# Rotary embedding over 16 batches: all transfers through one DMA ring, tables in 16 packets of 4 KB, slabs 2 and 3 stored as a pair

## The chip, the cores and the metric

The kernel runs on one core of a Trainium2 chip. A core has a matrix engine (PE), a vector engine (DVE, VectorE), a scalar engine (ACT, ScalarE), GpSimd (POOL) and a sync engine (SP, SyncE), and 16 DMA engines that move data between HBM and the on-chip memory of 128 partitions. SP and ACT each have a DMA ring of their own: a queue whose transfers are worked off in the order in which the engine issued them, spread over the 16 DMA engines. The metric is the device time of one execution in microseconds; the number that stands for a kernel is the median of its runs.

## What is computed

```python
batch, seq, dim = 16, 512, 1024        # num_heads = 16, head_dim = 64, half_dim = 32
x = x.reshape(batch, seq, num_heads, head_dim)
x1, x2 = x[..., :half_dim], x[..., half_dim:]
cos = cos[None, :, None, :]            # cos and sin: 512 x 32, float32
sin = sin[None, :, None, :]
rotated = np.concatenate([x1 * cos - x2 * sin,
                          x1 * sin + x2 * cos], axis=-1)   # float32
```

The input `x` is 33.55 MB and so is the output; the two tables are 64 KB each.

## The kernel before

**Tiling.** Two batches make a slab: 1024 rows of 1024 values, 4 MB. Two slabs make a pair. In a pair, partition p holds 16 consecutive rows, 64 KB; the first 32 KB belong to the even slab, the second 32 KB to the odd one. There are eight slabs and three places on chip for pairs (L52): pair 0 (slabs 0, 1) shares its place with pair 3 (slabs 6, 7), so slab 6 can be loaded only when slab 0 has been stored, and slab 7 when slab 1 has. A transfer of one slab is 128 packets of 32 KB, one of a pair 128 packets of 64 KB; `here` and `there` (L55, L59) give the two ends.

**Order of transfers.** On SP's ring stand all loads of `x`: load 0, load 1, slabs 2 and 3 as a pair in two halves (even partitions, then odd ones, L82), slabs 4 and 5 as a pair, and later, from inside the main loop (L168), load 6 and load 7. On ACT's ring stand the two tables (L78: 64 partitions of 1 KB each), and then all stores: slabs 0, 1, 2 and 3 one by one (L166), slabs 4 and 5 as a pair in two halves (L160), slabs 6 and 7 as a pair (L164). ACT issues a store between its own computing instructions.

**Tables.** GpSimd fills `pick` with zeros (L88) and sets ones or minus ones in it with four selects (L92). When the tables have landed, GpSimd casts them to bf16 (L99), PE multiplies them by `pick` (L106), which spreads the 64 rows over 128 partitions and gives the sign of the sine, and the two results `acc0` and `acc1` are cast into `tab0` on VectorE (L113) and `tab1` on ACT (L144).

**The main loop** runs over passes: slab 0 in two halves of four rows, slabs 1 to 6 whole, slab 7 in parts of 4, 2 and 2 rows. For each, ACT casts the float32 values to bf16 in the same place (L134), VectorE multiplies twice by the tables (L152) and adds (L155), and ACT copies the result back to float32 (L158). Casts run ahead of the copies: ACT's order is the cast of slab s+1, then the copy of slab s; from slab 6 on, all casts that are left come first. `copy` (L137) keeps ACT's order as written, and cast and copy both show up under L138.

Of the kernel before, what the change touches and what calls it, by code (L numbers as in the profile page):

```python
# [2 lines left out]

# [4 lines left out]


@with_exitstack  # L10
def kernel(
    ctx: ExitStack,
    tc: tile.TileContext,
    x: bass.AP,
    cos: bass.AP,
    sin: bass.AP,
    num_heads: int,
    out: bass.AP,
):
    nc = tc.nc  # L20
    P = nc.NUM_PARTITIONS

    batch, seq, dim = x.shape
    nh = num_heads
    hd = dim // nh
    half = hd // 2
    bf16 = mybir.dt.bfloat16
    f32 = mybir.dt.float32

    nb = 2  # L30
    nslabs = batch // nb
    rpp = nb * seq // P
    W = rpp * dim
    TP = seq // rpp
    TW = rpp * half

    out_flat = out.rearrange("b s h d -> b s (h d)")

    singles = ctx.enter_context(tc.tile_pool(name="singles", bufs=1))
    pairs = ctx.enter_context(tc.tile_pool(name="pairs", bufs=3))  # L40
    psum = ctx.enter_context(tc.tile_pool(
        name="psum", bufs=1, space=bass.MemoryType.PSUM))


    def view(t, offset, *dims):
        return dataclasses.replace(t, offset=t.offset + offset,
                                   ap=[t.ap[0], *[list(d) for d in dims]])

    places = [pairs.tile([P, 2 * W], f32, tag="pair", name="pair") for _ in range(3)]  # L52


    def here(s, n=1):  # L55
        return view(places[s // 2 % 3], s % 2 * W, (1, n * W))


    def there(t, s, n=1):  # L59
        return bass.AP(tensor=t.tensor, offset=t.offset + s // 2 * 2 * P * W + s % 2 * W,  # L60
                       ap=[[2 * W, P], [1, n * W]])


    def load(s, n=1):
        nc.sync.dma_start(out=here(s, n), in_=there(x, s, n))  # L65


    def store(s, n=1):
        nc.scalar.dma_start(out=there(out_flat, s, n), in_=here(s, n))  # L69


    load(0)


    cos_sb = singles.tile([TP, TW], f32, tag="cos_sb")
    sin_sb = singles.tile([TP, TW], f32, tag="sin_sb")
    for t, src in ((cos_sb, cos), (sin_sb, sin)):
        nc.scalar.dma_start(out=t, in_=bass.AP(  # L78
            tensor=src.tensor, offset=src.offset, ap=[[TW, TP], [1, TW]]))

    load(1)
    for p in range(2):  # L82
        nc.sync.dma_start(out=here(2, 2)[p::2], in_=there(x, 2, 2)[p::2])  # L83
    load(4, 2)


    pick = singles.tile([TP, 4 * P], bf16, tag="pick")
    nc.gpsimd.memset(pick, 0.0)  # L88
    for h in range(2):
        for g in range(2):  # L90
            part = view(pick, (2 * h + g) * P, (TP // 2, 2 * P // TP), (1, TP // 2))
            nc.gpsimd.affine_select(  # L92
                out=part, in_=part, compare_op=mybir.AluOpType.not_equal,
                fill=1.0 - 2.0 * g, base=-h, pattern=[[0, 2 * P // TP], [-2, TP // 2]],
                channel_multiplier=1)

    tab1 = singles.tile([TP, 2 * TW], bf16, tag="tab1")
    for i, t in enumerate((cos_sb, sin_sb)):
        nc.gpsimd.tensor_copy(out=view(tab1, i * TW, (1, TW)), in_=t)  # L99

    accs, tabs = [], []
    for h in range(2):
        acc = psum.tile([P, 2 * rpp * hd], f32, tag=f"acc{h}", name="acc")
        for i in range(2):
            for f in range(2):
                nc.tensor.matmul(  # L106
                    view(acc, i * rpp * hd + f * half, (hd, rpp), (1, half)),
                    view(pick, (2 * h + i * f) * P, (1, P)),
                    view(tab1, i * TW, (half, rpp), (1, half)),
                    start=True, stop=True)  # L110
        accs.append(acc)
        tabs.append(singles.tile([P, 2 * rpp * hd], bf16, tag=f"tab{h}", name="tab"))
    nc.vector.tensor_copy(out=tabs[0], in_=accs[0])  # L113

    passes = []
    for s in range(nslabs):
        r = 0  # L120
        for n in {0: (4, 4), nslabs - 1: (4, 2, 2)}.get(s, (rpp,)):
            passes.append((s, r, n))
            r += n


    def halves(u):
        s, r, n = u
        t = here(s).bitcast(bf16)
        return [view(t, (2 * r + i * n) * dim, (1, n * dim)) for i in range(2)]


    def cast(u):
        s, r, n = u
        copy(halves(u)[0], view(here(s), r * dim, (1, n * dim)))  # L134


    def copy(out, in_):  # L137
        tc.keep_in_program_order(nc.scalar.copy(out=out, in_=in_))  # L138


    ahead = list(passes)
    for _ in range(2):
        cast(ahead.pop(0))
    copy(tabs[1], accs[1])  # L144
    cast(ahead.pop(0))
    for i, u in enumerate(passes):
        s, r, n = u
        while ahead and len(passes) - len(ahead) < (i + 2 if s < nslabs - 2 else len(passes)):
            cast(ahead.pop(0))
        lo, up = halves(u)  # L150
        for t, a in ((up, 0), (lo, rpp * hd)):
            nc.vector.tensor_mul(  # L152
                out=t, in0=lo,
                in1=view(tabs[s % 2], a + r * hd, (hd, n), (0, nh), (1, hd)))
        nc.vector.tensor_add(  # L155
            out=up, in0=up, in1=view(lo, half, (hd, n * nh), (-half, 2), (1, half)))

        copy(view(here(s), r * dim, (1, n * dim)), up)  # L158
        if r + n == rpp:
            if s == 5:  # L160
                for p in range(2):
                    nc.scalar.dma_start(out=there(out_flat, 4, 2)[p::2], in_=here(4, 2)[p::2])  # L162
            elif s == 7:
                store(6, 2)  # L164
            elif s < 4:
                store(s)  # L166
            if s < 2:
                load(s + 6)  # L168


# [1 line left out]
_INS = ['x', 'cos', 'sin', 'num_heads']  # L172
_OUTS = [((16, 512, 16, 64), 'float32')]

_NUMBERS = {'num_heads': 16}


# [26 lines left out]
```

## Time and profile before

| | |
|---|---|
| median of 3 runs | 161.87 us (161.72 to 161.93) |
| the profiled run | 161.8 us, span 160.0 us |
| ACT casts and copies (L138) | 22 instructions, 112.1 us, 5155 ns each on average; 7.02 us for a whole slab |
| VectorE multiplies (L152) | 22 instructions, 71.4 us; 4.43 us for a whole slab |
| VectorE adds (L155) | 11 instructions, 35.8 us |
| cosine lands, cast on GpSimd | 0.74 + 11.1 us, 391 ns |
| sine lands, cast on GpSimd | 1.34 + 15.8 us, 396 ns |
| matmuls for the tables (L106) | 8, of which the last six take 1.43 us together |
| ACT starts slab 0, 1, 2, 4 | 13.35, 23.24, 44.49, 73.41 us |
| stores issued | 37.30, 58.47, 72.82, 87.38, 115.58, 116.14, 138.21 us |
| loads of slabs 6 and 7 issued | 69.8, 90.4 us |
| an issue of a DMA | 0.33 to 0.67 us on SP, 0.34 to 0.65 us on ACT |

The span is the time from the first to the last event that the profiler recorded on the core; the time of a run lies 1.8 us above it here. Stretches of the span are given in microseconds from its start. A transfer is recorded packet by packet; "lands" means the time at which its completion message arrives.

### The profile page before, as it was taken

The page shows a single profiled execution, that of the slowest core. Times are in us where ns is not written, and L with a number is a line of the kernel's source. Part 1 is how long each engine was busy: PE and PEld are TensorE (multiplying, and loading weights), DVE is VectorE, ACT ScalarE, POOL GpSimd, SP SyncE. Part 2 cuts the span into 40 slices and gives each one's busy share as a digit, 9 for nine tenths or more (in the row PEclk, how much of TensorE's full clock was granted, in tenths as well). Part 3 has the DMA queues.
Part 4 walks back from the last instruction along what each step waited for, and adds up shares of the span by engine and source line. Part 5 has one row for each costly group of instructions (what it writes and reads, how often), then busy time and mean ns, then how long its engine had stood idle before and what let it go on. Part 6 is the DMA issues. An engine that isn't in the chain of part 4 may idle for free.

```text
span 160.0 us, 167 instructions
## 1 busy us (share of the span) xinstructions
PE 2.0 (1%) x8; PEld 1.0 (1%) x8; DVE 107.9 (67%) x34; ACT 114.3 (71%) x24; POOL 2.6 (2%) x11
## 2 busy tenths in 40 slices
PE   0001300000000000000000000000000000000000
PEld 0000100000000000000000000000000000000000
DVE  0000499999951999799889979998999998000000
ACT  3006959993089989998998999999879999500000
POOL 4000000000000000000000000000000000000000
DMA  7999999699599999999999999999997999989966
GB/s 262 401 401 410 426 491 524 262 524 524 254 401 410 606 426 393 393 393 393 467 451 393 434 483 393 401 500 410 393 590 328 524 393 393 524 360 426 524 262 262
DMA packets 1920, 67.24 MB, mean 420 GB/s; under 512 B 256, under 2 KB 384, under 8 KB 384
## 3 DMA queue, kind: packets, MB, share of 16 engines
q1 hardware_dynamic: 880, 33.55, 49.5%
q10 hardware_dynamic: 1040, 33.69, 48.7%
HBM read 33.69 MB, written 33.55 MB: 420 GB/s over the span
## 4 chain that ended last, share of the span: by engine, by line
ACT 52%; DMA 26%; issue 5%; ACTq 1%; SPq 1%; another core or an unknown queue 0%
ACT pair L138 52%; DMA pair<-in_x_dram 26%; ACTq L162 1%; ACTq L69 1%; SPq L65 0%; SPq L83 0%; ACTq L138 0%
## 5 line engine op out<-in xcount | busy, mean ns | idle before, releaser
L138 ACT CAST pair<-pair 128x8192 bf16<-128x8192 f32 (+5 forms) x22 | 112.1, 5155 | 21.9 <-DMA pair<-in_x_dram 19.8
L152 DVE TENSOR_TENSOR pair<-pair,tab 128x8192 bf16<-128x8192 bf16 (+2 forms) x22 | 71.4, 3259 | 9.3 <-ACT pair L138 8.9
L155 DVE TENSOR_TENSOR pair<-pair 128x8192 bf16<-128x8192 bf16 (+2 forms) x11 | 35.8, 3260 | 0.3
L113 DVE CAST tab<-acc 128x1024 bf16<-128x1024 f32 x1 | 1.2, 1225 | 18.3 <-PE acc L106 18.3
L138 ACT ACT_TABLE_LOAD x1 | 1.3, 1283 | 2.0 <-issue 2.0
L106 PE MATMUL acc<-tab,pick 64*128 64x256 bf16 x8 | 2.0, 403 | 17.1 <-POOL tab L99 17.1
L106 PEld LDWEIGHTS <-pick 64*128 64x128 bf16 x8 | 1.0, 127 | 17.6 <-issue 15.6
L92 POOL TENSOR_SCALAR_AFFINE_SELECT pick<-pick 64x128 bf16<-64x128 bf16 x4 | 1.1, 303 | 0.1
L138 ACT CAST tab<-acc 128x1024 bf16<-128x1024 f32 x1 | 1.0, 1004 | 0.0
L99 POOL CAST tab<-cos_sb 64x256 bf16<-64x256 f32 x1 | 0.4, 391 | 9.5 <-DMA cos_sb<-in_cos_dram 9.5
L88 POOL MEMSET pick<- 64x512 bf16 x1 | 0.5, 519 | 0.3 <-POOLq L185 0.3
L99 POOL CAST tab<-sin_sb 64x256 bf16<-64x256 f32 x1 | 0.4, 396 | 4.9 <-DMA sin_sb<-in_sin_dram 4.9
L185 POOL MEMSET const-float32-0.0<- 128x1 f32 x1 | 0.1, 104 | 0.2 <-issue 0.2
L185 POOL MEMSET const-bfloat16-1.0<- 128x1 bf16 x1 | 0.1, 107 | 0.0
L185 POOL MEMSET const-uint8-127<- 128x1 uint8 x1 | 0.1, 107 | 0.0
L185 POOL MEMSET const-float32-1.0<- 128x1 f32 x1 | 0.1, 104 | 0.0
## 6 DMA issues: line engine op xcount, KB each, us to landing
pair<-in_x_dram SPq DMA_DIRECT2D x4, 4096.0 KB, 22.5
out_dram<-pair ACTq DMA_DIRECT2D x4, 4096.0 KB, 32.8
cos_sb<-in_cos_dram ACTq DMA_DIRECT2D x1, 64.0 KB, 11.1
sin_sb<-in_sin_dram ACTq DMA_DIRECT2D x1, 64.0 KB, 15.8
pair<-in_x_dram SPq DMA_DIRECT2D x3, 42.2
out_dram<-pair ACTq DMA_DIRECT2D x3, 21.0
```

The source lines that it names most:

```text
L69: nc.scalar.dma_start(out=there(out_flat, s, n), in_=here(s, n))
L88: nc.gpsimd.memset(pick, 0.0)
L92: nc.gpsimd.affine_select(out=part, in_=part, compare_op=mybir.AluOpType.not_equal, fill=1.0 - 2.0 * g, base=-h, pattern=[[0, 2 * P // TP] ...
L99: nc.gpsimd.tensor_copy(out=view(tab1, i * TW, (1, TW)), in_=t)
L106: nc.tensor.matmul(view(acc, i * rpp * hd + f * half, (hd, rpp), (1, half)), view(pick, (2 * h + i * f) * P, (1, P)), view(tab1, i * TW, ( ...
L113: nc.vector.tensor_copy(out=tabs[0], in_=accs[0])
L138: tc.keep_in_program_order(nc.scalar.copy(out=out, in_=in_))
L152: nc.vector.tensor_mul(out=t, in0=lo, in1=view(tabs[s % 2], a + r * hd, (hd, n), (0, nh), (1, hd)))
L155: nc.vector.tensor_add(out=up, in0=up, in1=view(lo, half, (hd, n * nh), (-half, 2), (1, half)))
L162: nc.scalar.dma_start(out=there(out_flat, 4, 2)[p::2], in_=here(4, 2)[p::2])
L185: nc = _bacc.Bacc("TRN2", target_bir_lowering=False, num_devices=1)
```

## The change

All transfers are issued by SP, in the order in which they stand in the program, with ACT issuing none.

- The tables are no longer laid over 64 partitions in packets of 1 KB. Each is cut into 16 rows of 4 KB, cosine in partitions 0, 8, 16, ..., sine in partitions 4, 12, 20, ... of one tile `raw` (128 partitions of 1024 float32 values), which VectorE fills with zeros first. They stand on SP's ring behind load 0 and ahead of load 1.
- GpSimd casts all of `raw` in one instruction. `pick` has 128 rows and six blocks, set by six selects. Each quarter of `acc` is now the sum of two matmuls over 128 rows, so there are 16 matmuls instead of 8.
- The load of slabs 4 and 5 moves from the start to behind store 0.
- Behind store 1 stand load 6 and load 7.
- Slabs 2 and 3 are stored as a pair, in two halves of 64 packets of 64 KB, when slab 3 is done; slabs 4 and 5 and slabs 6 and 7 as before.

So the ring's order is: load 0, cosine, sine, load 1, load 2-3 (two halves), store 0, load 4-5, store 1, load 6, load 7, store 2-3 (two halves), store 4-5 (two halves), store 6-7. The casts, multiplies, adds and copies of the main loop stay as they are.

```diff
     def load(s, n=1):
-        nc.sync.dma_start(out=here(s, n), in_=there(x, s, n))
+        tc.keep_in_program_order(nc.sync.dma_start(out=here(s, n), in_=there(x, s, n)))
     def store(s, n=1):
-        nc.scalar.dma_start(out=there(out_flat, s, n), in_=here(s, n))
+        tc.keep_in_program_order(
+            nc.sync.dma_start(out=there(out_flat, s, n), in_=here(s, n)))
+    TR = 16
+    TC = seq * half // TR
+    raw = singles.tile([P, TC], f32, tag="raw")
+    nc.vector.memset(raw, 0.0)
     load(0)
-    cos_sb = singles.tile([TP, TW], f32, tag="cos_sb")
-    sin_sb = singles.tile([TP, TW], f32, tag="sin_sb")
-    for t, src in ((cos_sb, cos), (sin_sb, sin)):
-        nc.scalar.dma_start(out=t, in_=bass.AP(
-            tensor=src.tensor, offset=src.offset, ap=[[TW, TP], [1, TW]]))
+    for i, src in enumerate((cos, sin)):
+        to = dataclasses.replace(
+            raw, offset=raw.offset + 4 * i * raw.ap[0][0],
+            ap=[[P // TR * raw.ap[0][0], TR], [1, TC]])
+        tc.keep_in_program_order(nc.sync.dma_start(out=to, in_=bass.AP(
+            tensor=src.tensor, offset=src.offset, ap=[[TC, TR], [1, TC]])))
     load(1)
     for p in range(2):
-        nc.sync.dma_start(out=here(2, 2)[p::2], in_=there(x, 2, 2)[p::2])
-    load(4, 2)
-    pick = singles.tile([TP, 4 * P], bf16, tag="pick")
+        tc.keep_in_program_order(
+            nc.sync.dma_start(out=here(2, 2)[p::2], in_=there(x, 2, 2)[p::2]))
+    pick = singles.tile([P, 6 * P], bf16, tag="pick")
     nc.gpsimd.memset(pick, 0.0)
-    for h in range(2):
-        for g in range(2):
-            part = view(pick, (2 * h + g) * P, (TP // 2, 2 * P // TP), (1, TP // 2))
+    for g in range(3):
+        for m in range(2):
+            part = view(pick, (g * 2 + m) * P + m, (2 * TR, P // TR // 2), (2, TR))
             nc.gpsimd.affine_select(
...
-    tab1 = singles.tile([TP, 2 * TW], bf16, tag="tab1")
-    for i, t in enumerate((cos_sb, sin_sb)):
-        nc.gpsimd.tensor_copy(out=view(tab1, i * TW, (1, TW)), in_=t)
+    raw_b = singles.tile([P, TC], bf16, tag="raw_b")
+    nc.gpsimd.tensor_copy(out=raw_b, in_=raw)
...
-        for i in range(2):
-            for f in range(2):
+        for g, at in ((0, 0), (0, half), (1, rpp * hd), (2, rpp * hd + half)):
+            for m in range(2):
                 nc.tensor.matmul(
-                    view(acc, i * rpp * hd + f * half, (hd, rpp), (1, half)),
-                    view(pick, (2 * h + i * f) * P, (1, P)),
-                    view(tab1, i * TW, (half, rpp), (1, half)),
-                    start=True, stop=True)
+                    view(acc, at, (hd, rpp), (1, half)),
+                    view(pick, (g * 2 + m) * P, (1, P)),
+                    view(raw_b, (2 * m + h) * TW, (half, rpp), (1, half)),
+                    start=m == 0, stop=m == 1)
...
         if r + n == rpp:
-            if s == 5:
+            if s == 7:
+                store(6, 2)
+            elif s > 1 and s % 2:
                 for p in range(2):
-                    nc.scalar.dma_start(out=there(out_flat, 4, 2)[p::2], in_=here(4, 2)[p::2])
-            elif s == 7:
-                store(6, 2)
-            elif s < 4:
+                    tc.keep_in_program_order(nc.sync.dma_start(
+                        out=there(out_flat, s - 1, 2)[p::2], in_=here(s - 1, 2)[p::2]))
+            elif s < 2:
                 store(s)
-            if s < 2:
-                load(s + 6)
+            if s == 0:
+                load(4, 2)
+            elif s == 1:
+                load(6)
+                load(7)
```

More of the change, by code (lines that the diff above doesn't have):

```diff
@@ L33 @@
     W = rpp * dim
-    TP = seq // rpp
     TW = rpp * half
@@ L92 @@
             nc.gpsimd.affine_select(
                 out=part, in_=part, compare_op=mybir.AluOpType.not_equal,
-                fill=1.0 - 2.0 * g, base=-h, pattern=[[0, 2 * P // TP], [-2, TP // 2]],
-                channel_multiplier=1)
-    tab1 = singles.tile([TP, 2 * TW], bf16, tag="tab1")
-    for i, t in enumerate((cos_sb, sin_sb)):
-        nc.gpsimd.tensor_copy(out=view(tab1, i * TW, (1, TW)), in_=t)
+                fill=-1.0 if g == 2 else 1.0, base=-4 if g else 0,
+                pattern=[[0, P // TR // 2], [-(P // TR), TR]], channel_multiplier=1)
```

## The prediction

> **What bounds the kernel now.** I read the page first: the span, engine totals and DMA rows.
>
> ```profile
> span 160.0 us, 167 instructions
> PE 2.0 (1%) x8; PEld 1.0 (1%) x8; DVE 107.9 (67%) x34; ACT 114.3 (71%) x24; POOL 2.6 (2%) x11
> ...
> DMA  7999999699599999999999999999997999989966
> ...
> q1 hardware_dynamic: 880, 33.55, 49.5%
> q10 hardware_dynamic: 1040, 33.69, 48.7%
> ```
>
> No engine passes 71%, while the packets of the two queues fill 49.5 + 48.7 = 98.2% of the 16 DMA engines' span. q1 is SyncE's ring (the loads, 33.55 MB), q10 ScalarE's (the stores and, from the 33.69, the two tables). The chain of waits hides this: it gives ACT 52% and DMA 26%, because it sees a transfer only where an engine waits for it.
>
> Then I cut the span where one row of packets ends on the first of the 16 engines and the next begins (a row: one packet on each engine). Columns: stretch, length, five engines' busy time, granted clock, DMA share, GB/s of packets that start inside.
>
> ```profile
> 1.96:3.77 1.81, 0.00 (x0) 0.00 (x0) 0.00 (x0) 1.28 (x1) 0.45 (x2) 1.00 0.51 199
> 3.77:22.62 18.85, 2.01 (x8) 0.92 (x7) 4.23 (x3) 8.02 (x3) 0.79 (x2) 1.00 1.04 440
> 22.62:39.54 16.92, 0.00 (x0) 0.00 (x0) 16.85 (x7) 14.04 (x3) 0.00 (x0) 1.00 1.02 434
> 39.54:42.52 2.98, 0.00 (x0) 0.00 (x0) 2.94 (x2) 0.00 (x0) 0.00 (x0) 1.00 0.64 242
> 42.52:119.93 77.41, 0.00 (x0) 0.00 (x0) 68.17 (x16) 72.70 (x11) 0.00 (x0) 1.00 1.01 437
> 119.93:139.29 19.36, 0.00 (x0) 0.00 (x0) 15.67 (x10) 18.24 (x7) 0.00 (x0) 1.00 1.01 437
> 139.29:160.00 20.71, 0.00 (x0) 0.00 (x0) 0.00 (x0) 0.00 (x0) 0.00 (x0) 1.00 0.87 377
> ```
>
> Loads alone (22.62 on) run at 434 GB/s, loads and stores mixed (42.52 on) at 437, stores alone (119.93 on) at 437. That is one ceiling: rings and direction don't change it. The same view cut into single rows gives the unit: a row of 64 KB packets takes 16.92 / 7 = 2.417 us, one of 32 KB 1.21.
>
> ```profile
> 17.75:18.96 1.21, 1.21 (x6) 0.57 (x4) 0.70 (x1) 1.21 (x1) 0.00 (x0) 1.00 1.01 433
> ...
> 37.13:39.54 2.41, 0.00 (x0) 0.00 (x0) 2.38 (x2) 0.14 (x1) 0.00 (x0) 1.00 1.16 435
> 39.54:42.52 2.98, 0.00 (x0) 0.00 (x0) 2.94 (x2) 0.00 (x0) 0.00 (x0) 1.00 0.64 242
> 42.52:43.73 1.21, 0.00 (x0) 0.00 (x0) 1.21 (x1) 0.00 (x0) 0.00 (x0) 1.00 1.01 433
> ...
> 136.83:139.29 2.46, 0.00 (x0) 0.00 (x0) 0.00 (x0) 1.35 (x1) 0.00 (x0) 1.00 1.05 453
> ```
>
> The sixteen slabs moved (eight in, eight out) are 64 rows of 64 KB: 64 x 2.417 = 154.7 us. All else the transfers lose is small and can be listed. (a) The first row takes 1.81 instead of 1.21: 0.60. (b) From 3.77 to 22.62 pass 15 rows of 32 KB, 15 x 1.21 = 18.15, in 18.85: the tables cost 0.70. (c) The row of loads during which the first store arrives takes 2.98 instead of 2.41: 0.57. (d) The last row before store 6-7 takes 2.46: 0.04. Sum: 1.96 + 154.7 + 0.60 + 0.70 + 0.57 + 0.04 = 158.6. The last store lands at 138.21 + 21.0 = 159.2, the span ends at 160.0, the profiled run's time is 161.8 and the median of the runs 161.87. So the change can win only out of (a) to (d), 1.9 us, and lose whatever it opens as a gap.
>
> **Part 1, the tables.** Before, 8 packets of 1 KB on each engine cost 0.70, or 0.088 each, of which 2.417 / 64 = 0.038 is data: 0.050 overhead. After, each engine gets 2 packets of 4 KB: 2 x 2.417 / 16 = 0.30 of data, and 0 to 2 x 0.050 overhead. I take the middle, 0.35: saved 0.70 - 0.35 = **0.35** (0.30 to 0.40).
>
> The Trainium skill ("DMA: Bandwidth & Descriptors", Rules for kernel authors) speaks against this: transfers under 64 KB are mostly overhead, and its fit gives about 2.0 us fixed for each DMA (for transfers from GpSimd). If both tables paid that inside the one ring, the sum would lose some 4 us. The trace goes against it where more is queued: 64 rows at 2.417, across all boundaries between transfers, leave only the 1.9 us listed.
>
> **Part 2, work for the tables.** VectorE fills `raw` at the start, and the tables' issue waits for that. No row shows this fill; bounds are POOL's 0.5 us (memset of 512 values) doubled and the 1.2 us of VectorE's L113 cast of 1024 values. Behind the wait stand the issues of the tables, load 1 and both halves of load 2-3, five of 0.4 to 0.7 us; load 0 keeps the ring full to 12.2, so the cost is 0. The masks on POOL grow from 4 selects of 303 ns to 6, and are done long before. GpSimd's cast goes from 256 values on 64 partitions (0.39 us) to 1024 on 128: four to eight times, 1.6 to 3.1. The matmuls for `acc0` go from 2 after the last cast (0.6 us) to 8, 1.9 us at the rate of the six at 17.64 (1.43 us) and 3.3 at 0.41 each. The tables land near 12.6 + 0.6 instead of 17.2, so VectorE's first multiply (19.58 now) comes between 17.9 and 20.8 (with L113's 1.2). At worst that is 1.2 late: slab 0's last add ends at 34.3 instead of 33.13, its last copy 3.6 later at 37.9 instead of 37.3, and store 0 is issued then; its ring has work to 41.6 and needs it at 40.4. Cost 0.
>
> **Part 3, one ring.** Loads 0-3 now run undisturbed to 1.96 + 1.81 + 7 x 1.21 + 0.35 + 4 x 2.417 + 8 x 2.417 = 41.6. Then, in ring order with 9.67 for a slab and 19.33 for a pair: store 0 to 51.3, load 4-5 to 70.6, store 1 to 80.3, load 6 to 89.9, load 7 to 99.6, store 2-3 to 119, store 4-5 to 138.3, store 6-7 to 157.6, all up to 0.57 later if (c) stays. What could open a gap is an issue that comes late. From issue to first row takes 1.2 us (0.74 to 1.96; 138.21 to 139.29 is 1.1), from last row to landing 0.65 (158.6 to 159.2).
>
> ACT starts slab 2 at 41.6 + 0.65 = 42.3 instead of 44.49. Two casts and copies of 13.94 each end at 56.2 (store 1, needed at 69.4) and 70.2. Slab 4 lands at 71.5 instead of 73.41, so 1.9 is won; ACT no longer pauses 0.41 to issue store 3, and slab 6's multiply starts 2.3 earlier, 106.4. From there VectorE sets the pace. Store 2-3 is ready at 85.4, needed at 98.4; store 4-5 at 113.3, needed at 117.8; store 6-7 at 138.2 - 2.3 = 135.9, needed at 137.1: the smallest margin, 1.2. SP's queue blocks once on a transfer: load 7 waits for store 1 to land, 81.0, and is needed at 88.7; behind it stand only store 2-3 and later, so nothing is held up. So (d) goes: **0.04**. Eight 64 KB rows for sixteen of 32 KB at stores 2-3 give 8 x (2 x 1.21 - 2.417), **0.02**.
>
> **Part 4, loss (c).** It ends in a load's row, while the first store's own row takes a clean 1.21. Either it comes from a store ring joining running loads; then it goes, 0.57 saved. Or it is the price of the first store; then it stays, 0 saved. The rows speak for both: the lengthened row is the load's, but in the 77.41 us after it, load 7's ring joins running stores with no such loss. No row is nearer to one end; I take half, **0.28**.
>
> **Sum.** 0.35 + 0.04 + 0.02 + 0.28 = 0.69 off: 161.87 - 0.69 = **161.2**; 160.9 if (c) goes, 161.5 if it stays.
>
> **Rivals.** *Only the tables' part comes through*: 161.5, 0.41 less. For it: a first write can be slow wherever it is queued. Against: the store's own row is not longer.
>
> *Turning round inside one ring costs.* In the trace a ring never goes from loads to stores without idling. The new ring turns three times to stores and twice back to loads (51, 80). If the engines don't fetch across a turn, each turn to a load pays the start-up of (a), 0.60, and each to a store (c)'s 0.57: 2 x 0.60 + 3 x 0.57 = 2.91, less the old 0.57 and the 0.41: +1.9, **163.8**. With only the two turns to loads: 162.1 to 162.7. It decides from 0.2 us a turn on (0.98 / 5). Against it: in the mixed stretch every engine turns at nearly each row and still makes 437 GB/s; but there another ring supplies the next packet.
>
> On this, the Trainium skill ("DMA: Bandwidth & Descriptors", Two DMAs through the same engine are not ordered) says that a queue's descriptors start in order but are pipelined, with reads and writes on separate queues. By that no turn costs; no row here shows it for a mixed ring.
>
> *The tables stop the ring.* Each now stands alone in the stream with one packet per engine, and nothing beside it. If each pays the start-up of (a), that is 2 x 0.60 = 1.2: 162.4. Against it: load 0 to load 1 and all later boundaries cost nothing visible. This is what would be left of the skill's rule.
>
> *The last store comes late.* If slab 4 lands, or the end of ACT's work comes, more than 1.2 us behind my schedule, the ring runs dry before store 6-7, and each further us costs one. With no gain over before at 138.2, the gap is 1.1: 161.2 + 1.1 = 162.3.
>
> **Chances.** Forecast (160.8 to 161.4) 0.47; only the tables' part (161.4 to 161.7) 0.26; turns 0.17; tables stop the ring 0.03; late last store 0.07. Less than 0.2%, 0.32 us, can't be told from no change here, so faster is below 161.55. Faster: 0.47 and 0.10 of the 0.26 = 0.57. Same: the other 0.16. Slower: 0.17 + 0.03 + 0.07 = 0.27. The range goes from 160.7 to 162.8, leaving out the full price of the turns and a little below, under 0.2; the forecast's own is 160.8 to 161.5.
>
> **What would show it.** Right: one DMA queue with 98% or more of the span; slab 2's cast near 42.3, slab 4's near 71.5, last copy near 136, the last store landing near 158.5. (c) is read from the row after load 2-3. Wrong: stretches around 41.6, 51, 71, 80 and 100 below 430 GB/s (turns), or a hole before the last 8 MB (late store).

## The result, and the profile after

The changed kernel takes 162.56 us (median of 9 runs, 161.95 to 163.49) against 161.87 for the kernel before (9 runs beside it, 161.72 to 162.24): ratio 1.0044, 95% interval 1.0028 to 1.006. It is slower by 0.7 us where 0.7 less was forecast. Ratios and intervals, here and below, are worked out from the fast runs alone, so a ratio need not be the quotient of the two medians beside it. The profiled run, at 161.95 us, is the fastest of the nine; two further sets of runs of the same kernel (below, `again` and `third`) left traces of 162.48 and 162.57 us, and the readings use these as well.

The page of the changed kernel: span, engine totals, the DMA engines in 40 slices, the queue, the chain's summary.

```profile
span 160.2 us, 194 instructions
PE 3.4 (2%) x16; PEld 2.3 (1%) x16; DVE 108.7 (68%) x35; ACT 114.0 (71%) x24; POOL 3.3 (2%) x12
...
DMA  7999999799699897999999999996997997997992
...
q1 hardware_dynamic: 1696, 67.24, 98.0%
...
DMA 34%; ACT 29%; DVE 12%; issue 8%; ACTq 2%; SPq 1%
```

One queue carries all, 98.0% of the span, and no slice inside is empty: nothing here looks wrong. The chain again names the DMA engines only where somebody waits for them.

The timeline, at the points that the schedule had named (start, length, engine and line, idle time before):

```profile
18.00 8.96 DVE L157 TENSOR_TENSOR pair<-pair,tab 128x4096 bf16<-128x4096 bf16 x4
...
37.35 0.35 SPq L70 DMA_DIRECT2D out_dram<-pair  x1
...
43.21 27.78 ACT L143 CAST pair<-pair 128x8192 bf16<-128x8192 f32 x4 [5.89 <-DMA pair<-in_x_dram]
...
72.26 55.65 ACT L143 CAST pair<-pair 128x8192 bf16<-128x8192 f32 x10 [1.27 <-DMA pair<-in_x_dram]
...
136.54 0.35 SPq L70 DMA_DIRECT2D out_dram<-pair  x1
```

The schedule held. Slab 2 starts 1.3 us earlier than before (44.49), slab 4 1.2 earlier (73.41), and store 6-7 is issued at 136.54 instead of 138.21, in time for its turn at 138.9. The compute engines gave what was asked of them; the time went in the DMA engines.

Two places show it. The first is the row of loads ahead of store 0. The same cuts for both kernels: seven rows of load 2-3, then its last row, up to the first packet of store 0. First the kernel before, then the changed kernel, then `third`.

```profile
22.38:39.30 16.92, 0.00 (x0) 0.00 (x0) 16.85 (x7) 14.04 (x3) 0.00 (x0) 1.00 1.00 434
39.30:42.28 2.98, 0.00 (x0) 0.00 (x0) 2.94 (x2) 0.00 (x0) 0.00 (x0) 1.00 1.02 352
```

```profile
22.27:39.20 16.93, 0.00 (x0) 0.00 (x0) 16.90 (x7) 14.04 (x3) 0.00 (x0) 0.50 1.00 434
39.20:42.16 2.96, 0.00 (x0) 0.00 (x0) 2.93 (x2) 0.00 (x0) 0.00 (x0) 0.50 1.00 354
```

```profile
22.09:39.03 16.94, 0.00 (x0) 0.00 (x0) 16.91 (x7) 14.03 (x3) 0.00 (x0) 1.00 1.00 433
39.03:42.45 3.42, 0.00 (x0) 0.00 (x0) 3.39 (x2) 0.00 (x0) 0.00 (x0) 1.00 1.00 307
```

The loads run at 434 GB/s in all three. The last row takes 2.98, 2.96 and 3.42 instead of 2.42. Loss (c) did not go, and in `third` it is 1.0. On average over the 16 engines (by the packet records, a packet's time less 2.418) it is 0.61 before, 0.55 in the changed kernel's trace, 1.13 in `again` and 1.02 in `third`. Note what `third` does: it comes to this row 0.27 us earlier than the kernel before (39.03 against 39.30) and leaves it 0.17 later.

The second place is the end. Cut into half microseconds, the last stretch shows when each of the 16 engines starts its last packet of 64 KB: one such start in 0.5 us reads as 131 GB/s, sixteen as 2097. Kernel before, then `third`:

```profile
156.00:156.50 0.50, 0.00 (x0) 0.00 (x0) 0.00 (x0) 0.00 (x0) 0.00 (x0) 1.00 4.84 2097
156.50:157.00 0.50, 0.00 (x0) 0.00 (x0) 0.00 (x0) 0.00 (x0) 0.00 (x0) 1.00 0.00 0
157.00:157.50 0.50, 0.00 (x0) 0.00 (x0) 0.00 (x0) 0.00 (x0) 0.00 (x0) 1.00 0.00 0
```

```profile
156.00:156.50 0.50, 0.00 (x0) 0.00 (x0) 0.00 (x0) 0.00 (x0) 0.00 (x0) 1.00 2.72 1180
156.50:157.00 0.50, 0.00 (x0) 0.00 (x0) 0.00 (x0) 0.00 (x0) 0.00 (x0) 1.00 1.51 655
157.00:157.50 0.50, 0.00 (x0) 0.00 (x0) 0.00 (x0) 0.00 (x0) 0.00 (x0) 1.00 0.60 262
```

Before, all 16 engines start their last packet within half a microsecond. In `third` nine do, five come in the next half and two after 157.0. The last store's completion comes 0.3 to 0.4 us after the last of these packets ends (158.85 and 159.2 before, 159.59 and 159.9 in `third`), so the late engines set the time. By the packet records the engines' ends lie 0.40 us apart before, and 0.75, 0.94 and 1.00 in the three traces of the changed kernel; the mean end moved only from 158.59 to 158.55, 158.91 and 158.95. (The records don't number the engines; a packet is put behind the one at whose end it starts.)

### The profile page after: what moved, and what is told of

The parts are those of the page before. It is cut to its first block, busy times and chain, and to the rows that moved or that the text cites. A ratio compares the mean times of both kernels' runs of the same rounds, so it can differ in the third digit from the quotient of the medians.

```text
span 160.2 us, 194 instructions
## 1 busy us (share of the span) xinstructions
PE 3.4 (2%) x16; PEld 2.3 (1%) x16; DVE 108.7 (68%) x35; ACT 114.0 (71%) x24; POOL 3.3 (2%) x12
## 4 chain that ended last, share of the span: by engine, by line
DMA 34%; ACT 29%; DVE 12%; issue 8%; ACTq 2%; SPq 1%
DMA pair<-in_x_dram 34%; ACT pair L143 29%; DVE pair L157 10%; ACTq L208 1%; DVE pair L160 1%; SPq L83 1%; DVE raw L77 1%; SPq L70 0%; ACTq L143 0%
## 5 line engine op out<-in xcount | busy, mean ns | idle before, releaser
L111 PE MATMUL acc<-raw_b,pick 128*128 128x256 bf16 x16 | 3.4, 403 | 14.8 <-POOL raw_b L104 14.8
L111 PEld LDWEIGHTS <-pick 128*128 128x128 bf16 x16 | 2.3, 146 | 15.5 <-issue 12.8
L77 DVE MEMSET raw<- 128x1024 f32 x1 | 0.9, 912 | 1.0 <-PEq L194 1.0
L98 POOL TENSOR_SCALAR_AFFINE_SELECT pick<-pick 128x64 bf16<-128x64 bf16 x6 | 1.3, 263 | 0.1
L104 POOL CAST raw_b<-raw 128x1024 bf16<-128x1024 f32 x1 | 1.0, 1037 | 10.8 <-DMA raw<-in_sin_dram 10.8
L94 POOL MEMSET pick<- 128x768 bf16 x1 | 0.7, 738 | 0.3 <-POOLq L194 0.3
```

Of the source, the lines that this page charges most:

```text
L77: nc.vector.memset(raw, 0.0)
L98: nc.gpsimd.affine_select(out=part, in_=part, compare_op=mybir.AluOpType.not_equal, fill=-1.0 if g == 2 else 1.0, base=-4 if g else 0, pat ...
L104: nc.gpsimd.tensor_copy(out=raw_b, in_=raw)
L111: nc.tensor.matmul(view(acc, at, (hd, rpp), (1, half)), view(pick, (g * 2 + m) * P, (1, P)), view(raw_b, (2 * m + h) * TW, (half, rpp), (1 ...
```

## The experiments

Every kernel stands beside runs of the kernel before on the same chip. "Turns" counts how often a ring goes from loads to stores.

| kernel | rings, tables | turns | median | before | ratio (95%) |
|---|---|---|---|---|---|
| changed kernel | one, 4 KB packets in it | 3 | 162.56 | 161.87 | 1.0044 (1.0028 to 1.006) |
| again | the same | 3 | 162.58 | 161.76 | 1.0039 (1.0004 to 1.0074) |
| third | the same | 3 | 162.34 | 161.79 | 1.0041 (1.0022 to 1.0061) |
| three_turns | the same | 2 | 162.14 | 161.76 | 1.0021 (0.9997 to 1.0045) |
| four_turns | the same | 4 | 162.86 | 161.79 | 1.0078 (1.005 to 1.0106) |
| one_ring_old_tables | one, 1 KB packets in it | 3 | 161.97 | 161.76 | 1.0014 (1.0003 to 1.0026) |
| old_tables_again | the same | 3 | 162.29 | 161.94 | 1.0017 (1.0003 to 1.0032) |
| old_two_turns | the same | 2 | 161.68 | 161.79 | 1.0001 (0.999 to 1.0013) |
| tables_act | one, 4 KB packets on ACT's | 3 | 162.13 | 161.78 | 1.0024 (1.0013 to 1.0036) |
| tables_act2 | the same | 3 | 162.13 | 161.79 | 1.0019 (1.0005 to 1.0033) |
| tables_only | two, 4 KB packets | none | 161.90 | 161.94 | 0.9999 (0.9984 to 1.0015) |
| two_rings | two, 4 KB packets, pair store | none | 166.30 | 161.76 | 1.0299 (1.0263 to 1.0334) |
| early_after | as changed, small store first | 3 | 162.84 | 161.94 | 1.005 (1.0032 to 1.0068) |
| early_before | as before, small store first | none | 164.17 | 161.94 | 1.0129 (1.0105 to 1.0153) |
| copy_many | one, none | 6 | 164.03 | 161.78 | 1.013 (1.0103 to 1.0158) |
| copy_few | one, none | 2 | 161.98 | 161.78 | 1.0011 (1.0002 to 1.002) |
| copy_two_rings | two, none | none | 161.97 | 161.78 | 1.0008 (0.9999 to 1.0017) |

(three_turns counts its two turns to stores and its one back.)

### The changed kernel again

> The changed kernel once more, for a second trace and its spread. Two theories. TURNS: in a ring that carries both directions, each turn from loads to stores stops each of the 16 DMA engines for a time of its own, and what the slowest has lost by the end is the loss. TABLES: the two table transfers, alone in the ring between load 0 and load 1, cost more than the 0.35 us that they were to save. Both: 162.2 to 162.9, ratio 1.002 to 1.006. TURNS: the last landing's spread over the 16 engines differs from the first trace's 0.75 us and is the larger the slower the run, with the rows next to loads-to-stores boundaries lengthened; TABLES: the rows from 12 to 22 us carry the loss and the later ones are clean. If neither, the ratio is 1.000 and the first comparison was the chip's.

162.58 us, ratio 1.0039: the loss is real. The lengthened row and the spread at its end are as told above for `third` (1.13 on average, and 0.94). The stretch from load 0 to load 2-3, where TABLES saw the loss, is shorter than before, not longer (load 2-3 starts on average at 22.31 instead of 22.57).

### The stores on their own ring

```diff
 def store(s, n=1):
-            nc.sync.dma_start(out=there(out_flat, s, n), in_=here(s, n)))
+            nc.scalar.dma_start(out=there(out_flat, s, n), in_=here(s, n)))
```

(and the same in the stores of pairs)

> The changed kernel with the stores on ACT's ring; tables in 16 packets of 4 KB, pair store of slabs 2-3 and order of loads as changed. TURNS: no ring carries both directions, so the loss goes and what the tables save is left: 161.4 to 161.8, ratio 0.997 to 1.000. TABLES: the same loss as the changed kernel, 162.2 to 162.9, ratio 1.002 to 1.006.

166.30 us: neither. The timeline and the cuts of this kernel say why:

```profile
116.56 1.51 ACTq L169 DMA_DIRECT2D out_dram<-pair  x2
118.56 4.43 DVE L160 TENSOR_TENSOR pair<-pair 128x8192 bf16<-128x8192 bf16 x1
121.29 21.23 ACT L143 CAST pair<-pair 128x4096 bf16<-128x4096 f32 x7 [4.76 <-DMA pair<-in_x_dram]
```

```profile
136.60:139.05 2.45, 0.00 (x0) 0.00 (x0) 2.05 (x2) 2.45 (x2) 0.00 (x0) 1.00 0.99 428
139.05:143.39 4.34, 0.00 (x0) 0.00 (x0) 0.00 (x0) 3.47 (x2) 0.00 (x0) 1.00 0.00 0
143.39:145.84 2.45, 0.00 (x0) 0.00 (x0) 0.00 (x0) 0.00 (x0) 0.00 (x0) 1.00 1.00 428
```

With two rings an engine takes one packet from each in turn. Slabs 2-3 are stored here in packets of 64 KB, load 7 comes in packets of 32 KB, so the store gets two thirds of the engines; ACT waits 4.76 us for slab 7, store 6-7 is issued at 142.55, and for 4.34 us no packet starts. So the pair store of slabs 2-3 and the one ring belong together, and the time of this run says nothing about turns. Its trace does, at the first store (the rows of load 2-3 and the row ahead of store 0, cut as above):

```profile
22.18:39.11 16.93, 0.00 (x0) 0.00 (x0) 16.90 (x7) 14.03 (x3) 0.00 (x0) 1.00 1.00 434
39.11:42.31 3.20, 0.00 (x0) 0.00 (x0) 3.17 (x2) 0.00 (x0) 0.00 (x0) 1.00 1.05 328
```

No ring turns here, and yet that row loses 0.93 on average over the engines, nearly as much as in `again` and `third`. The long row ahead of store 0 is therefore not the price of a turn inside a ring; the kernel before, with two rings, has it as well (0.61).

### Fewer turns

```diff
+    load(4, 2)
...
-            if s == 0:
-                load(4, 2)
-            elif s == 1:
+            if s == 1:
                 load(6)
                 load(7)
```

The added line stands behind load 2-3.

> The changed kernel, one ring, but load 4-5 stands at the start as before, so that store 0 and store 1 follow each other: two turns to stores (after load 4-5, after load 7) instead of three, one back to loads instead of two. TURNS: part of the loss goes: 161.8 to 162.3, ratio 1.000 to 1.003. TABLES: as the changed kernel, 162.2 to 162.9.

162.14 us, ratio 1.0021, about half the loss, as TURNS had it; but the interval, 0.9997 to 1.0045, holds both no loss and the changed kernel's, so this run alone does not decide. The row ahead of its first store, now at 58 us, still loses 0.86 on average.

### One ring with the tables of before

The table code of the kernel before (L75 to L110), with its two transfers on SP's ring behind load 0; all else as changed.

> All transfers in one ring in the changed order, but with the tables of before (64 partitions of 1 KB each, four packets on each engine, old masks and eight matmuls). TURNS: as slow as the changed kernel or up to 0.4 slower, 162.3 to 163.0, ratio 1.003 to 1.008. TABLES: if the 4 KB packets are what costs, this one is no slower than before, 161.6 to 162.0, ratio 0.998 to 1.001.

> One ring with the tables of before, a second time, for a second trace: 161.8 to 162.3. If its row ahead of store 0 is again only 0.2 to 0.3 us too long (1.1 and 0.9 in two of the kernels with the new tables), the new tables and the stop at the first store belong together; if it is 0.6 or more, that stop simply differs from run to run.

161.97 and 162.29 us, ratios 1.0014 and 1.0017: slower than before, but by less than TURNS expected. So there are two parts: one ring costs some 0.15%, the 4 KB tables inside it some 0.25% more. The row ahead of store 0 is 0.31 and 0.43 too long on average over the engines; the second lies between the two marks of its expectation (up to 0.3, and 0.6 or more).

### The new tables alone

Kernel before, its two rings and its order, with the new table code on ACT's ring.

> The kernel before with only the new tables (16 packets of 4 KB each, the new masks and 16 matmuls), on ACT's ring as before; order, rings and stores as before. TABLES (the new tables make the kernel slower by themselves): 162.0 to 162.6, ratio 1.002 to 1.005. TURNS (they are harmless where no ring carries both directions): 161.4 to 161.8, ratio 0.997 to 1.000, with 0.1 to 0.3 less in the stretch from 3 to 22 us.

0.9999: the tables cost nothing, and win nothing, where the loads of `x` and the stores have a ring each. Load 2-3 starts at 22.58 (22.57 before), and the 0.1 to 0.3 us that were expected there did not show. The row ahead of store 0 loses 0.65 on average, here too with two rings.

### Is it the first store, wherever it stands?

```diff
     load(0)
+    z = singles.tile([P, P], f32, tag="z")
+    nc.gpsimd.memset(z, 0.0)
+    nc.scalar.dma_start(
+        out=bass.AP(tensor=out_flat.tensor, offset=out_flat.offset + 3 * 2 * P * W,
+                    ap=[[P // 16 * 2 * W, 16], [1, P]]),
+        in_=dataclasses.replace(z, ap=[[P // 16 * z.ap[0][0], 16], [1, P]]))
```

> The changed kernel, and at the start one small store more, from ACT's ring: 16 rows of 512 B of zeros into the rows of slab 6, which store 6-7 writes over at the end. Traces so far: the row of loads ahead of store 0 lasts 0.2 to 1.1 us too long, later turns 0.02 to 0.1. FIRST STORE (the stop is the price of a kernel's first store, wherever it stands): the stop moves to the start, the row ahead of store 0 falls to 2.42 to 2.6, and the time to 161.4 to 162.2 if the early stop hides in the wait for the first load. TURN (the stop belongs to a long run of loads giving way to stores): the row ahead of store 0 stays at 2.9 to 3.6 and the time at 162.2 to 163.0.

> The kernel before with the same small early store on ACT's ring ahead of the tables. FIRST STORE: the 0.57 us of the row ahead of store 0 goes or moves, 161.2 to 161.7. TURN: unchanged, 161.7 to 162.0.

`early_after` takes 162.84 us and its row ahead of store 0 is still 1.02 too long on average: a small write beforehand does not take the loss away. That does not make it the turn, though. The small store went through ACT's ring and store 0 through SP's, so the first store of each ring remains a rival, and `two_rings` shows the loss without a turn in either ring. `early_before`, where both stand on ACT's ring, is spoiled: the sine stood behind the small store and was cast at 19.84 instead of 17.20, store 0 was issued at 39.51 instead of 37.30, and ACT later waited 3.67 us for slab 7. Its row ahead of store 0 loses nothing (0.01 on average), but so does that of `tables_act2` (0.01), which has no early store; so it does not decide between the two.

### Turns by themselves

```diff
 # copy_many
+    for s in range(3):
+        load(s)
+    for s in range(5):
+        store(s)
+        load(s + 3)
+    for s in range(5, 8):
+        store(s)
```

> A bare copy of x to out through one ring, slab by slab, all tables and arithmetic left out: loads 0 to 2, then store 0, load 3, store 1, load 4 and so on to load 7, then stores 5 to 7. It turns six times from loads to stores and five times back, with single slabs of 9.7 us between. So far the turn after 40 to 60 us of loads cost an engine 0.3 to 1.1 us on average, those after 19 us 0.03 to 0.2. If each turn to stores costs something by itself, six times 0.05 to 0.2 shows in the rows before the stores and the copy is 0.3 to 1.0 us slower than copy_few; if only the first long run of loads counts, the first turn (after 29 us) costs 0.2 to 0.8 and the others nothing. Either way 159.5 to 161.5.

> The same copy in one ring with two turns to stores and one back: loads 0 to 5, stores 0 to 5, loads 6 and 7, stores 6 and 7. If a turn's cost grows with the run of loads ahead of it, the first one (after 58 us) costs 0.8 to 1.3 and the second (after 19) 0.03 to 0.2: 159.5 to 161.

> The same copy, order of copy_many, with stores on ACT's ring: loads and stores take turns packet by packet from the first landing on. One start of stores beside loads, after about 12 us: 0 to 0.6 there and nothing later, 0.3 to 1.0 below copy_many if turns in one ring cost, equal to it if not.

These kernels leave out the tables and all arithmetic; the loops shown take the place of everything behind `store`. They take 164.03 (4 runs), 161.98 and 161.97 us; the first two had been expected at 161.5 or less. In all three, the rows of loads at the first store lose 1.0 to 1.3 in sum on average over the engines, with two rings (1.04) as with one. The same bytes, one ring: four more turns each way cost 2.05 us, twice the upper end of what was expected. `copy_two_rings` has the order of `copy_many` and differs only in the ring of its stores; it takes 2.06 us less. That is the price of one ring with six turns. The end of `copy_many`, in starts of 32 KB packets (one in 0.5 us reads as 66 GB/s; columns are length, POOL, clock, DMA share, GB/s):

```profile
157.50:158.00 0.50, 0.00 (x0) 1.00 1.67 721
158.00:158.50 0.50, 0.00 (x0) 1.00 0.61 262
158.50:159.50 1.00, 0.00 (x0) 1.00 0.08 33
159.50:160.00 0.50, 0.00 (x0) 1.00 0.15 66
```

Eleven engines start their last packet in the first half microsecond and four in the second; the single starts behind them are the last two packets of one engine, which ends 1.5 us behind the last of the others (161.08 against 159.59 by the packet records). The packet records show where it fell back: at the later turns, the engines that come first to the end of the loads lose little or nothing and the ones that come last lose most. At the turn at 71 us the last two lost 0.08 each; at 90 us the first seven lost at most 0.08, the next eight 0.06 to 0.22, the last 0.44. At 110 and 130 us the late engine, by then about a packet behind, lost 0.36 and 0.78 in one packet. In these rows nothing brings a late engine back. (A spread by itself is no sign of turns: in `copy_two_rings`, which has none, the ends lie 0.94 apart, and in `copy_few` 0.55, at the same time.)

### Four turns in the kernel, and two with the old tables

```diff
 # four_turns
-            if s == 0:
-                load(4, 2)
-            elif s == 1:
-                load(6)
-                load(7)
+            if s == 0:
+                load(4)
+            elif s == 1:
+                load(5)
+                load(6)
+            elif s == 2:
+                load(7)
```

(stores 2 and 3 one by one)

> The changed kernel, one ring, with one more turn each way: after load 2-3 come store 0, load 4, store 1, loads 5 and 6, store 2, load 7, store 3, store 4-5, store 6-7 (slabs 2 to 5 moved one by one where the order needs it); four turns to stores instead of three, three back instead of two. By the schedule every load still lands ahead of its cast and every store is issued before its turn. If turns are the cost, 162.6 to 163.4 and above the changed kernel of this call by 0.1 to 0.6; if not, level with it.

> One ring, the tables of before, load 4-5 at the start: two turns to stores. With three turns and these tables the ratio was 1.0014 and 1.0017; with two and the new tables 1.0021. If turns are the cost: 1.000 to 1.0015, 161.7 to 162.1.

1.0078 and 1.0001. With the new tables two, three and four turns give 1.0021, 1.0041 (the middle of three) and 1.0078; with the old ones two and three give 1.0001 and 1.0016. Neighbouring intervals overlap in part, but the order is the same in both series. The profiled run of `four_turns` was its slowest, 164.21 us; its end looks like that of `copy_many` (one engine starts its last packet after 158.5), and shows what one late engine can cost, not the usual run:

```profile
156.00:156.50 0.50, 0.00 (x0) 0.00 (x0) 0.00 (x0) 0.00 (x0) 0.00 (x0) 1.00 2.72 1180
156.50:157.00 0.50, 0.00 (x0) 0.00 (x0) 0.00 (x0) 0.00 (x0) 0.00 (x0) 1.00 1.21 524
157.00:158.50 1.50, 0.00 (x0) 0.00 (x0) 0.00 (x0) 0.00 (x0) 0.00 (x0) 1.00 0.30 131
158.50:159.00 0.50, 0.00 (x0) 0.00 (x0) 0.00 (x0) 0.00 (x0) 0.00 (x0) 1.00 0.31 131
```

### The place of the tables

```diff
-        tc.keep_in_program_order(nc.sync.dma_start(out=to, in_=bass.AP(
+        tc.keep_in_program_order(nc.scalar.dma_start(out=to, in_=bass.AP(
```

> The changed kernel with its two table transfers (16 packets of 4 KB each) on ACT's ring, nothing else on that ring. One ring lost 0.0014 to 0.0017 with the old tables and 0.0039 to 0.0044 with the new ones, while the new tables cost nothing with two rings (0.9999). If it is their place in the ring that adds the rest, this gives 161.9 to 162.3, ratio 1.001 to 1.002; if it is the work behind them (masks, 16 matmuls, layout) or chance, 162.4 to 162.9, ratio 1.003 to 1.006.

> The changed kernel a third time, to stand beside the other three on one chip: 162.3 to 162.7, ratio 1.003 to 1.005.

> The changed kernel with its tables on ACT's ring a second time (1.0024 before). If the place of the tables in the ring adds to the loss, 161.9 to 162.3 and below the changed kernel of this call by 0.2 to 0.6; if the first difference was chance, level with it.

1.0024 and 1.0019 against 1.0041 beside them: out of the ring the new tables are 0.2% cheaper, on the same chip 0.21 us, though the intervals overlap. The traces show where. The first cut is `tables_act2`, seven rows of load 2-3 and the row ahead of store 0:

```profile
22.68:39.61 16.93, 0.00 (x0) 0.00 (x0) 16.86 (x6) 14.03 (x3) 0.00 (x0) 0.50 1.00 434
39.61:42.06 2.45, 0.00 (x0) 0.00 (x0) 2.42 (x2) 0.00 (x0) 0.00 (x0) 0.50 1.02 441
```

It comes to that row 0.58 us later than `third` (39.61 against 39.03) and leaves it 0.39 us earlier. Over all traces, on average over the 16 engines: where the 4 KB tables stand in the one ring (six traces), load 2-3 starts at 22.31 to 22.52, mean 22.38, and the row ahead of store 0 loses 0.55 to 1.13, mean 0.95. In one ring with the tables elsewhere or in 1 KB packets (five traces) it starts at 22.69 to 22.91, mean 22.75, and the row loses 0.01 to 0.43, mean 0.25. So 0.37 us are won ahead of load 2-3 and 0.70 lost ahead of the first store; the difference, 0.33, is the 0.2% between the kernels.

This is not a matter of the one ring. The four two-ring kernels fall in with the rest: load 2-3 starts at 22.34 in `two_rings`, 22.57 before, 22.58 in `tables_only` and 22.79 in `early_before`, and the row ahead of store 0 loses 0.93, 0.61, 0.65 and 0.01. Over all 15 traces with tables, each 0.1 us by which load 2-3 starts earlier goes with some 0.2 us more lost ahead of the first store (correlation -0.96), whether that store comes at 42 us or at 60. So what is won at the tables is lost again, and more. Why, no run here tells. It stays open.

## Why the prediction was wrong

**What bounds the kernel** was right: a stream of DMA rows at one rate, 433 to 437 GB/s, whatever the direction, with some 2 us beside it. Two things were read too coarsely. My cuts stood 0.24 us behind the first engine's packets (the first packet starts at 1.73 and not 1.96), which moves no length in the sum. And I cut on the first of 16 engines and treated a row as one thing; the end is set by the last engine, and the view by rows was blind to that.

**Part 1** had the right mechanism and too large a size: 0.35 saved was forecast; in the three traces of the changed kernel load 2-3 starts at 22.52, 22.31 and 22.32 against 22.57, 0.05 to 0.26 saved. The rule of the Trainium skill ("DMA: Bandwidth & Descriptors", Anatomy of one DMA — SWDGE (gpsimd) path), some 2 us fixed for each transfer issued from GpSimd, does not show in the rows of a full ring fed by SP: with both tables between load 0 and load 1, load 2-3 still starts earlier than before.

**Part 2** held at zero. VectorE's fill took 0.91 us, the cosine was issued at 1.96, GpSimd's cast took 1.04 (2.7 times the smaller cast and not four to eight times, so below my bounds of 1.6 to 3.1), VectorE's first multiply came at 18.00, inside 17.9 to 20.8.

**Part 3** held. Slab 2 came at 43.21 for 42.3, slab 4 at 72.26 for 71.5, late by 0.9 and 0.8 us; store 6-7 was issued at 136.54 with its turn at 138.9, and no hole opened. Of the 0.9, 0.55 is the long row ahead of store 0, of which the schedule for slab 2 had nothing, and 0.30 what the tables did not save. The rival of the late last store did not happen.

**Part 4 is the step that failed**, together with its silent zero for the later turns. The text gave (c) two ends, "then it goes, 0.57 saved" and "then it stays, 0 saved", and took the half, 0.28 saved. The first end needed a store ring that joins running loads; with one ring none joins, and the row ahead of store 0 is long all the same. An end at which (c) grows was missing. Measured alike on average over the engines, it was 0.61 before and 0.55, 1.13 and 1.02 in the three traces of the changed kernel: 0.06 saved once, 0.52 and 0.41 lost twice. It grows where load 2-3 starts early, with or without a turn, so Part 1's saving and (c) were not independent terms to be added. The sign that the prediction named for turns, a stretch around 41.6 below 430 GB/s, could not tell: it reads 354 and 307 after, and 352 before.

The later turns, which the sum held at nothing, cost 0.07 to 0.24 on average over the engines and left them further apart at the end, 0.75 to 1.00 us instead of 0.40. For `third` the account closes by packet records to 0.05: mean end of the engines 158.95 against 158.59, 0.36 later (row ahead of store 0 0.41 longer, later turns 0.24, load 2-3 0.24 earlier), and the last engine 0.64 behind the mean instead of 0.26, 0.38 more: 0.74 together; the two profiled runs lie 0.77 apart (162.57 against 161.80).

**The rival "Turning round inside one ring costs"** was right in kind for the later turns: `copy_many` against `copy_two_rings` shows it, 2.06 us. Its prices were wrong. Turns back to loads cost next to nothing here (the rows of load 4-5 behind store 0 last 2.418 to 2.428 on average in the three traces), turns to stores cost the late engines most, and (c), which it charged for each turn to a store, is lost ahead of the first store with or without a turn. Five turns at 0.57 to 0.60, 163.8, is too dear for the kernel. The argument against it, that mixed rows in two rings run at 437 GB/s, was true and did not apply: with two rings an engine has both directions at hand (`copy_two_rings`, 161.97 us), with one ring all engines change over within a row or two.

The sentence of the Trainium skill ("DMA: Bandwidth & Descriptors", Two DMAs through the same engine are not ordered) that descriptors of a queue are pipelined, with reads and writes on separate queues, fits the turns back to loads. For the turns to stores I drew from it that they cost nothing; the measurement decides otherwise, 2.05 us for four more of them in `copy_many`.

Why the late engines lose at the later turns is not shown: that they still load while the others already store is what the records have in common, and no run took the one without the other.

## What to carry to other kernels

When a stream of transfers fills the DMA engines, look at when each of the 16 ends, not at when the stream does: a half microsecond hides in the slowest engine while rates and busy shares look perfect. Keep loads and stores on separate rings unless the order of one ring pays for its turns from loads to stores; with two rings, give packets that must share the engines the same size. A gain early in the stream counts only if a later boundary doesn't take it back, so terms of one stream are not to be added without a look at that.

## What was not expected of the hardware

A bare copy of the same bytes, with no tables and no arithmetic, takes 161.97 us with two rings and 161.98 with two turns in one, no less than the kernel before: in these orders the bytes alone take as long as the whole kernel. The best one-ring version, `old_two_turns`, is level with the kernel before (1.0001). With both rings busy, one packet goes to each ring in turn whatever its size: 1 KB of the tables and 32 KB of load 0 alternate from 6 to 10 us in the kernel before, and in `two_rings` 64 KB and 32 KB alternate almost throughout from 93 to 119 us, so that the 64 KB ones get two thirds. The granted TensorE clock was 0.57 in eight of the nine runs of the changed kernel and 1.00 in the ninth, which was the slowest: its 16 short matmuls are done by 18.2 us, and in `third` the medians at the two clocks are alike (162.35 at 1.00, 162.33 at 0.57), so the clock has no part in this that the runs show.
